# RG-LRU block 2's second half by seven products, and a third head without a block: a change to a hybrid trunk kernel

## The chip, the cores and the metric

The kernel runs on one core of a Trainium2 chip. The metric is the device time of one execution in microseconds (us). The median of three runs of the kernel before is 1455.85 us (1454.58 to 1456.62).

## What is computed

One step of a decoder layer on 2048 prompt tokens and 8 sample tokens of width 1024. In short:

```python
hn = rmsnorm(x, g_norm) * (1 + scale) + shift       # scale, shift, gate from silu(c) @ w_ada + b_ada
xa, za, q, k, v, glr, zg = split(hn @ w_in)
# RG-LRU group, 8 blocks of 128 channels
xc = conv4(xa); gx, ga = sigmoid(blockdiag(xc))      # gates, one 128x128 matrix a block
a = exp(8 * ga * log_sigmoid(lam)); u = sqrt(1 - a*a) * gx * xc
h[t] = a[t] * h[t-1] + u[t]; y_lru = h * silu(za)
# GLA group, 4 heads of 128 keys and 256 values
S[t] = diag(alpha[t]) S[t-1] + k[t]^T v[t]; o[t] = q[t] S[t]
y_gla = rmsnorm_per_head(o) * silu(zg)
x = x + gate * (concat(y_lru, y_gla) @ w_out); y = rmsnorm(x, g_final)
```

All is float32. Results are the outputs of both token groups and the new states (recurrent, convolution, GLA).

## The kernel before

**Precision.** A float32 product is made of three matmuls of split operands: high by high, high by low, low by high. So one projection of 128 columns of w_in on n tokens is 8 x 3 = 24 matmuls of 128 x n (`project`, L661 to L663).

**Two halves.** The 2048 tokens are worked in two halves of 1024. In each half the four GLA heads run in the order HEADS = (3, 0, 1, 2). After a head come the RG-LRU blocks given to it: in the first half all eight (LRU_TILES: block 0, then 1 and 2, then 3 and 4, then 5 to 7), in the second half the first block of each entry of LATE_TILES; blocks 6 and 7 of the second half run with the start of the out-projection. A half is cut into segments of tokens (SEGS): two of 512 in the first half, 384, 384 and 256 with the 8 samples (264) in the second. The samples of a block run with its second half, save for the blocks in EARLY, whose samples run in the first half, in segments of 512, 256 and 264 (SAMPLES; chosen in `xa_load`).

**Seven products.** For the second half's gate columns of three heads (`gates_seven`) and for the blocks in EARLY (`lru_seven`), a pair of 128-column groups on 1024 tokens is not made by `project` but by a seven-product scheme (`seven`): seven products of 12 matmuls of 128x512 each (`product`, L1561) and additions on DVE. The combinations of weights that it needs are made ahead by `pair_weights`, one pair after another, and kept in DRAM (`twd`). This stage stands between the two halves, in the order gates_seven(0), lru_seven(0), gates_seven(1), lru_seven(1), gates_seven(2).

**The order.** The instruction streams of the engines are given by the order in which Python emits them. Each engine executes its stream in order. Work that shall lie beside matmuls is put off: `after(units, fn)` puts a function on a heap, due some units later, and `tick()`, called after every projection or value tile, advances the clock and runs what is due. The GLA's recurrence works so: `chunks` runs one 128-token chunk (`gla_chunk`), and puts off the next by PACE. `new_values` empties the heap of the recurrence's entries before a head's value tiles are written, since the value tiles vh and vl hold one head at a time.

**Background work.** `pair_weights` comes first; after the last pair, `out_weights` makes the combinations for the out-projection in 16 steps (0 to 15): POOL loads r (L829), DVE multiplies and combines (L850), and in some steps b22 and t are split on ACT and DVE into p (L854, L855); POOL stores r, t (L864) and p (L857). Each step puts off the next by 4 units. It pauses at the stage between the halves and goes on after it. The tiles r, t, p and g are in the pool `hp`. After the last head the rest of it is run (`while outw["busy"]`), then the pools `gp` and `hp` are closed, and the out-projection's pools use their places: `load_w` (L1710) loads the first weights by SP, `hi_part` (L1696, ACT) and `lo_part` (L1699, DVE) split them. A tile in a reused place waits for the last readers and writers of what it overlaps.

**A block.** `xa_unit` projects a segment, ACT copies it to xa (L1394), ACT and DVE do the convolution (cv, L1276 and L1278), `split` or the lines after it make xh on ACT and xl on DVE (L1295 and L1296, or L1302 and L1303). Two or three units later `gates` runs six matmuls on xh and xl (L1315 to L1317) with two activations (L1318); after the last segment come ACT's exponentials (L1323 to L1326), DVE's tg, tx (L1331, L1332), the scan over 1024 tokens (L1334) and the sample step. `out` multiplies by silu(za) (L1352) and `spill` stores it (L675, L679). At a head's end `gla_out` transposes the normalized chunks (L1162; L1164 for the samples) and DVE multiplies by the gate (L1167).

The lines of the out-projection's matmuls are L1846. After the change the line numbers rise by 2 to 12.

Of the kernel before, what the change touches and what calls it, by code (L numbers as in the profile page):

```python
# [33 lines left out]
PAD, PAD_XP = 16, 32  # L34
SEGS = (((0, 512), (512, 512)), ((0, 384), (384, 384), (768, 264)))
SAMPLES = ((0, 512), (512, 256), (768, 264))
EARLY = (0, 1)
LATE_TILES = ((2,), (3,), (4,), (5, 6, 7))
HEADS = (3, 0, 1, 2)
LRU_TILES = ((0,), (1, 2), (3, 4), (5, 6, 7))  # L40
PACE = ((1, 1), (1, 0.75, 1.5))
ZB11, ZT1, ZT2, ZB21, ZT3, ZB22, ZT4 = range(7)

CTS = (8, 0)
# [10 lines left out]
def hybrid_kernel(ctx, tc, i, o):  # L55
# [506 lines left out]
    def first_head():  # L562

        h = HEADS[0]
        n = DV + RANK
        v = vh, vl = new_values()

        def evict(tt, ps, low=None):
            hi, lo = vh[tt // 4][:, tt % 4], vl[tt // 4][:, tt % 4]
            S.copy(hi, ps[:, :DV])  # L570
            turn48 = low_rank(ps[:, DV:n], slice(0, P), tt * P, st)

            def lower():
                V.tensor_tensor(lo, ps[:, :DV], hi.bitcast(F32), op=OP.subtract)
            if low is None:
                lower()
            else:
                low.append(lower)
            return turn48

        def second(g, u, low=True):
            x = xt0[4 + 2 * g:6 + 2 * g]
            return apply(turn(x, (2 * u, 2 * u + 1)), 4 + 2 * g, (2 * u, 2 * u + 1), 2, low)

        def pair(a, kts):
            for kt in range(*kts):
                for tt in (a, a + 1):
                    if tt not in begun:
                        begun[tt] = acc()
                    value_mm(begun[tt][:, :n], slice(tt * P, (tt + 1) * P), wv0, n, (kt, kt + 1))  # L590

        with in_order():
            ranks = []
            ss = squares(st, xt0[4:6], P, "junk")
            split_parts(1)
            rs = scales(st, ss, 2)
            split_parts(1)
            times(xt0[4:6], rs)
            low = []
            for tt in range(4):  # L600
                value_mm(begun[tt][:, :n], slice(tt * P, (tt + 1) * P), wv0, n, (6, KT))
                ranks.append(evict(tt, begun[tt], low))
# [24 lines left out]
            second(1, 2)  # L627
            second(1, 3)
            pair(4, (4, KT))
            ranks = [evict(tt, begun[tt]) for tt in (4, 5)]  # L630
            pair(6, (0, KT))
            ranks += [evict(tt, begun[tt]) for tt in (6, 7)]
        store_parts()
        with tc.issue_after(last[V.engine]), tc.issue_after(last[S.engine]):
            normalize(st, [xsr], NS, "junk")

        def rest():
            for f in ranks:
                f()
        return v, prep, rest  # L640
# [57 lines left out]
    pend = []  # L698
    clock = [0, 0]

    def after(units, fn, gla=False, val=False):
        clock[1] += 1
        heapq.heappush(pend, (clock[0] + units, clock[1], fn, gla, val))

    def tick(units=1.0):
        clock[0] += units
# [197 lines left out]
    def sample_values(h, w, n):  # L904

        n4 = n // 4
        vs = gp.tile([P, DV], F32, tag="os", name="vs")
        ps = acc()
        for kt in range(KT):
            raw = w[kt // 4]  # L910
            for g in range(4):
                PE.matmul(ps[32 * g:32 * g + NS, :n4], fs[:, kt], raw[:, kt % 4, g * n4:(g + 1) * n4],
                          start=kt == 0, stop=kt == KT - 1)
        for g in range(4):
            r = slice(32 * g, 32 * g + NS)
            (S.copy if g % 2 else V.tensor_copy)(vs[r, :min(n4, DV - g * n4)], ps[r, :min(n4, DV - g * n4)])
        for g in range(4):
            c = slice(g * n4, min((g + 1) * n4, DV))
            G.dma_start(vsd[h][:, c], vs[32 * g:32 * g + NS, :c.stop - c.start])
        if n > DV:  # L920
            r = slice(96, 96 + NS)
            return low_rank(ps[r, DV - 3 * n4:n4], r, TH)
        return lambda: None

    def new_values():
        while any(e[4] for e in pend):
            e = min(e for e in pend if e[3])
            pend.remove(e)
            heapq.heapify(pend)
            e[2]()  # L930
        return [[gp.tile([P, 4, DV], F32R, tag=tag, name=tag, bufs=2) for _ in range(2)] for tag in ("vh", "vl")]

    def values(half, h, w):
        first = h == HEADS[0]
        n = DV + (RANK if first else 0)
        vh, vl = new_values()
        turns = []
        for tt in range(8):
            if half == 1 and tt == first:
                with held(V) if first else ExitStack():  # L940
                    raw = raw_values(h, n)
            if tt == 4:
                while drips:
                    drip()
            if half == 0 or tt < 6:
                ps = acc()
                value_mm(ps[:, :n], slice(tt * P, (tt + 1) * P), w, n, (0, KT))
            elif tt == 6:
                both = [acc(), acc()]
                for k in (0, 4):  # L950
                    for m in range(2):
                        value_mm(both[m][:, :n], slice((6 + m) * P, (7 + m) * P), w, n, (k, k + 4))
                ps = both[0]
            else:
                ps = both[1]
            hi, lo = vh[tt // 4][:, tt % 4], vl[tt // 4][:, tt % 4]
            S.copy(hi, ps[:, :DV])  # L957
            V.tensor_tensor(lo, ps[:, :DV], hi.bitcast(F32), op=OP.subtract)  # L958
            if len(turns) == 3 or tt == 7 and turns:
                turns.pop(0)()  # L960
            if first:
                turns.append(low_rank(ps[:, DV:n], slice(0, P), tt * P))
            tick(0.5)
        if half == 1:
            turns.append(sample_values(h, raw, n))
        for f in turns:
            after(1, f, True)
        return vh, vl
# [201 lines left out]
    def gla_head(half, h, wv=None, ahead=None):  # L1170
# [15 lines left out]
        def chunks(s, c):  # L1186

            nch = min(SEGS[half][s][1], TH - SEGS[half][s][0]) // P
            if c == 0:
                prep[s, "run"] = gla_start(half, h, s, prep[s])  # L1190
                after(PACE[half][0], lambda: chunks(s, 1), True, True)
                return
            if c == nch and half:
                gate_load(s)
            gla_chunk(half, h, s, c - 1, prep[s], prep[s, "run"], v)
            if c < nch:
                after(PACE[half][1], lambda: chunks(s, c + 1), True, True)
                return
            gla_norm(nch, prep[s, "run"])
            after(PACE[half][2] if half else 1 if s + 1 < ns else 2, lambda: finish(s), True)  # L1200
            if s + 1 < ns:
                after(0, lambda: chunks(s + 1, 0), True, True)
            elif half == 1:
                G.dma_start(o[4][0, 0, h], St[h])

# [22 lines left out]
        for s in range(ns):  # L1228
# [10 lines left out]
            if s + 1 < ns:  # L1239
                dec = gla_decay(half, h, s + 1)  # L1240
            if s == 0:
                after(2 if h == HEADS[0] else 1, lambda: chunks(0, 0), True, True)
            tick()
        if half == 1:
            after(1, lambda: sample(prep[2][3], 0), True)
# [418 lines left out]
            lru_last_a(LRU_TILES[k])  # L1664
    gates_ahead(HEADS[0])
    gates_seven(0)
    for n in range(2):
        lru_seven(n)
        gates_seven(1 + n)
    while drips:  # L1670
        drip()
    close_sp()
    for k, h in enumerate(HEADS):
        wx = []
        gla_head(1, h, ahead=lambda: wx.extend(weights(XA + LATE_TILES[k][0] * P, P)))
        lru(1, LATE_TILES[k][:1], wx)
    flush_gla()
    while outw["busy"]:
        heapq.heappop(pend)[2]()
    gpx.close()  # L1680
    hpx.close()

# [577 lines left out]
```

## Time and profile before

| | us |
|---|---|
| median of 3 runs | 1455.85 |
| profiled execution | 1454.69 |
| its span | 1452.9 |
| PE busy | 1424.1 |
| DVE busy | 1051.5 |
| ACT busy | 689.6 |
| POOL busy | 220.0 |

The span goes from the first to the last instruction that the profiler recorded; 1.8 us of the execution lie around it. PE is TensorE's matmuls, PEld its weight loads, DVE is VectorE, ACT ScalarE, POOL GpSimd, SP SyncE; a q behind an engine's name is its queue, which issues DMAs. A row of a timeline gives start, duration, engine, line, operation, output and inputs, shape, count, and in brackets how long the engine had been idle and what ended it. Matmuls overlap one another: the time that one takes on PE is the distance between starts, not its duration.

The stages by time: first half to about 600 us, the seven products from 603 to 708, the second half to about 1076 (the last head's sample transposes), blocks 6 and 7 to about 1127, then the out-projection to the end.

### The profile page before, as it was taken

The page shows a single profiled execution, that of the slowest core. Times are in us where ns is not written, and L with a number is a line of the kernel's source. Part 1 is how long each engine was busy: PE and PEld are TensorE (multiplying, and loading weights), DVE is VectorE, ACT ScalarE, POOL GpSimd, SP SyncE. Part 2 cuts the span into 40 slices and gives each one's busy share as a digit, 9 for nine tenths or more (in the row PEclk, how much of TensorE's full clock was granted, in tenths as well). Part 3 has the DMA queues.
Part 4 walks back from the last instruction along what each step waited for, and adds up shares of the span by engine and source line. Part 5 has one row for each costly group of instructions (what it writes and reads, how often), then busy time and mean ns, then how long its engine had stood idle before and what let it go on. Part 6 is the DMA issues. An engine that isn't in the chain of part 4 may idle for free. (4 is left out here: it accounts for less than half of the span.)

```text
span 1452.9 us, 23584 instructions
## 1 busy us (share of the span) xinstructions
PE 1424.1 (98%) x8741; PEld 1250.8 (86%) x8741; DVE 1051.5 (72%) x2477; ACT 689.6 (47%) x1251; POOL 220.0 (15%) x364
## 2 busy tenths in 40 slices
PE   7999999999999999999999999999999999999998
PEld 5888989899898988778999999999998887788886
DVE  5757657776676688955468687586788986688886
ACT  4644544662545358524353454535557622144342
POOL 0200111212122113100212322323100000000000
PEclk9999999999999999999999999999999999999999
DMA  9755775764666455667846565656562767694453
GB/s 328 268 185 175 260 262 203 249 236 165 199 209 203 148 179 207 207 221 237 292 158 201 186 217 184 220 186 209 184 226 83 276 221 272 232 362 131 139 171 116
DMA packets 161752, 305.33 MB, mean 210 GB/s; under 512 B 12962, under 2 KB 91458, under 8 KB 159197
## 3 DMA queue, kind: packets, MB, share of 16 engines
q1 hardware_dynamic: 106837, 217.39, 43.6%
q0 software_dynamic: 22752, 70.44, 14.3%
q10 hardware_dynamic: 32048, 16.00, 3.7%
q8 instruction: 69, 1.13, 0.3%
q14 instruction: 46, 0.38, 0.1%
HBM read 188.51 MB, written 115.33 MB: 209 GB/s over the span
## 5 line engine op out<-in xcount | busy, mean ns | idle before, releaser
L661 PE MATMUL acc<-hh,w 128*128 128x512 f32 (+3 forms) x1112 | 386.1, 347 | 0.5 <-DVE xb L999 0.2
L662 PE MATMUL acc<-hl,w 128*128 128x512 f32 (+3 forms) x1112 | 375.6, 338 | 0.2 <-DVE hl L205 0.2
L663 PE MATMUL acc<-hh,w 128*128 128x512 f32 (+3 forms) x1112 | 375.1, 337 | 0.0
L662 PEld LDWEIGHTS acc<-hl,w 128*128 128x128 f32 x1112 | 209.3, 188 | 18.1 <-issue 1.2
L661 PEld LDWEIGHTS acc<-hh,w 128*128 128x128 f32 x1112 | 209.2, 188 | 18.1 <-ACT tx L1318 0.9
L663 PEld LDWEIGHTS acc<-hh,w 128*128 128x128 f32 x1112 | 209.1, 188 | 16.3
L1846 PE MATMUL acc<-w,a 128*128 128x512 f32 (+1 forms) x792 | 184.8, 386 | 0.0
L1846 PEld LDWEIGHTS acc<-w,a 128*128 128x128 f32 x792 | 146.8, 188 | 33.2 <-issue 3.4
L346 PE MATMUL acc<-w,hh 128*128 128x256 f32 (+1 forms) x508 | 144.7, 285 | 0.0
L348 PE MATMUL acc<-w,hl 128*128 128x256 f32 (+1 forms) x508 | 143.5, 282 | 0.2 <-DVE hl L228 0.2
L347 PE MATMUL acc<-w,hh 128*128 128x256 f32 (+1 forms) x508 | 143.4, 282 | 0.0
L1846 PE MATMUL tp<-w,a 128*128 128x512 f32 x564 | 136.0, 391 | 0.0
L1846 PEld LDWEIGHTS tp<-w,a 128*128 128x128 f32 x564 | 105.2, 188 | 26.8 <-issue 5.2
L346 PEld LDWEIGHTS acc<-w,hh 128*128 128x128 f32 x508 | 95.5, 188 | 1.3 <-ACT zs L1128 0.4
L348 PEld LDWEIGHTS acc<-w,hl 128*128 128x128 f32 x508 | 96.2, 189 | 0.4 <-DVE hl L228 0.4
L347 PEld LDWEIGHTS acc<-w,hh 128*128 128x128 f32 x508 | 96.0, 189 | 0.2
L1128 ACT ACTIVATE zs<-acc 128x512 f32<-128x512 f32 (+3 forms) x70 | 34.3, 490 | 107.0 <-PE acc L663 104.0
L1696 ACT CAST a<-s 128x512 fp32r<-128x512 f32 x61 | 36.5, 619 | 96.1 <-issue 36.6
L1278 DVE SCALAR_TENSOR_TENSOR cv<-xa,vecT,cv 128x512 f32<-128x512 f32 (+2 forms) x120 | 76.3, 638 | 7.2 <-ACT cv L1276 6.7
L1129 DVE SCALAR_TENSOR_TENSOR zs<-zs,acc 128x512 f32<-128x512 f32 (+3 forms) x70 | 38.4, 548 | 46.7 <-ACT zs L1128 46.7
L957 ACT CAST vh<-acc 128x256 fp32r<-128x256 f32 x56 | 20.5, 369 | 94.2 <-PE acc L348 81.8
L958 DVE TENSOR_TENSOR vl<-acc,vh 128x256 fp32r<-128x256 f32 x56 | 23.3, 420 | 51.1 <-ACT vh L957 51.1
(403 smaller groups left out, 2746.4 us busy)
## 6 DMA issues: line engine op xcount, KB each, us to landing
parts<-w SPq DMA_DIRECT2D x37, 1024.0 KB
w<-parts SPq DMA_DIRECT2D x28, 1024.0 KB
wr<-in_w_in_dram SPq DMA_DIRECT2D x38, 512.0 KB
a<-mixd SPq DMA_DIRECT2D x63, 256.0 KB
w<-wd SPq DMA_DIRECT2D x12, 1024.0 KB
w<-twd SPq DMA_DIRECT2D x20, 512.0 KB
mixd<-zs ACTq DMA_DIRECT2D x34, 256.0 KB
wada<-in_w_ada_dram SPq DMA_DIRECT2D x16, 512.0 KB
```

The lines of the kernel that those rows point to most:

```text
L346: PE.matmul(ps, hh[:, kt, c], hi[:, kt % 4], start=kt == 0, stop=False)
L347: PE.matmul(ps, hh[:, kt, c], lo[:, kt % 4], start=False, stop=False)
L348: PE.matmul(ps, hl[:, kt, c], hi[:, kt % 4], start=False, stop=kt == KT - 1)
L661: PE.matmul(ps[:, :n], hi[:, kt], a, start=kt == 0, stop=False)
L662: PE.matmul(ps[:, :n], hi[:, kt], b, start=False, stop=False)
L663: PE.matmul(ps[:, :n], lo[:, kt], a, start=False, stop=kt == KT - 1)
L958: V.tensor_tensor(lo, ps[:, :DV], hi.bitcast(F32), op=OP.subtract)
L1128: S.activation(z, ps, AF.Tanh, scale=0.5)
L1129: V.scalar_tensor_tensor(z, z, 1.0, ps, op0=OP.add, op1=OP.mult)
L1278: V.scalar_tensor_tensor(cv[:, cq], xa[:, cq.start + k:cq.stop + k], cw[k], cv[:, cq], op0=OP.mult, op1=OP.add)
L1696: S.copy(t[:, 0, k], (low(t) if src is None else src)[:, k])
L1846: PE.matmul(ps, t[:, u, k], w[:, v, k, c], start=(q < 3 or ps is own) and (k, u, v) == (0, 0, 0), stop=(k, u) == (3, 1), skip_group_check= ...
```

## The change

Four things change together:

- EARLY gets block 2: its second half is made by the seven products, so there are six pairs of weights in place of five, and its samples run in the first half.
- LATE_TILES gives blocks 3, 4, none, and 5 to 7 to the four heads of the second half. The third head (head 1) has no RG-LRU block.
- `new_values` is called for each half of a head's value tiles, and only drains the recurrence as far as that half's place needs: four chunks of the head before for tiles 0 to 3, eight for tiles 4 to 7 (`chunked` counts them). So the last four chunks of a head can stand between the next head's first value tiles. PACE's second half has 0.5 units between chunks in place of 0.75.
- Places: the samples' value tile vs moves from the pool `gp` to `xp`, and a small tile pads `gp` before it is closed.

```diff
-EARLY = (0, 1)
-LATE_TILES = ((2,), (3,), (4,), (5, 6, 7))
+EARLY = (0, 1, 2)
+LATE_TILES = ((3,), (4,), (), (5, 6, 7))
-PACE = ((1, 1), (1, 0.75, 1.5))
+PACE = ((1, 1), (1, 0.5, 1.5))
...
-        vs = gp.tile([P, DV], F32, tag="os", name="vs")
+        vs = xp.tile([P, 512], F32, tag="f512", name="vs")[:, :DV]
...
-    def new_values():
-        while any(e[4] for e in pend):
+    chunked = [8]
+
+    def new_values(v, g):
+
+        while chunked[0] < 4 * g + 4:
             e = min(e for e in pend if e[3])
             pend.remove(e)
             heapq.heapify(pend)
             e[2]()
-        return [[gp.tile([P, 4, DV], F32R, tag=tag, name=tag, bufs=2) for _ in range(2)] for tag in ("vh", "vl")]
+        for x, tag in zip(v, ("vh", "vl")):
+            x.append(gp.tile([P, 4, DV], F32R, tag=tag, name=tag, bufs=2))
...
-        vh, vl = new_values()
+        v = vh, vl = [], []
         turns = []
         for tt in range(8):
+            if tt % 4 == 0:
+                new_values(v, tt // 4)
...
             gla_chunk(half, h, s, c - 1, prep[s], prep[s, "run"], v)
+            chunked[0] += 1
...
             if s == 0:
-                after(2 if h == HEADS[0] else 1, lambda: chunks(0, 0), True, True)
+                chunked[0] = 0
+                after(2 if h == HEADS[0] else 1, lambda: chunks(0, 0), True)
...
-    for n in range(2):
+    for n in EARLY:
         lru_seven(n)
-        gates_seven(1 + n)
+        if n < 2:
+            gates_seven(1 + n)
...
     for k, h in enumerate(HEADS):
-        wx = []
-        gla_head(1, h, ahead=lambda: wx.extend(weights(XA + LATE_TILES[k][0] * P, P)))
-        lru(1, LATE_TILES[k][:1], wx)
+        wx, js = [], LATE_TILES[k][:1]
+        gla_head(1, h, ahead=js and (lambda: wx.extend(weights(XA + js[0] * P, P))))
+        lru(1, js, wx)
     flush_gla()
     while outw["busy"]:
         heapq.heappop(pend)[2]()
+    gp.tile([P, 24], F32, name="pad")
     gpx.close()
     hpx.close()
```

More of the change, by code (lines that the diff above doesn't have):

```diff
@@ L565, in first_head @@
         n = DV + RANK
-        v = vh, vl = new_values()
+        v = vh, vl = [], []
+        for g in range(2):
+            new_values(v, g)
         def evict(tt, ps, low=None):
@@ L699, in hybrid_kernel, with after @@
     clock = [0, 0]
-    def after(units, fn, gla=False, val=False):
+    def after(units, fn, gla=False):
         clock[1] += 1
-        heapq.heappush(pend, (clock[0] + units, clock[1], fn, gla, val))
+        heapq.heappush(pend, (clock[0] + units, clock[1], fn, gla))
     def tick(units=1.0):
@@ L935, in values @@
         n = DV + (RANK if first else 0)
-        vh, vl = new_values()
+        v = vh, vl = [], []
         turns = []
         for tt in range(8):
+            if tt % 4 == 0:
+                new_values(v, tt // 4)
             if half == 1 and tt == first:
@@ L1190, in chunks @@
                 prep[s, "run"] = gla_start(half, h, s, prep[s])
-                after(PACE[half][0], lambda: chunks(s, 1), True, True)
+                after(PACE[half][0], lambda: chunks(s, 1), True)
                 return
@@ L1195, in chunks @@
             gla_chunk(half, h, s, c - 1, prep[s], prep[s, "run"], v)
+            chunked[0] += 1
             if c < nch:
-                after(PACE[half][1], lambda: chunks(s, c + 1), True, True)
+                after(PACE[half][1], lambda: chunks(s, c + 1), True)
                 return
@@ L1201, in chunks @@
             if s + 1 < ns:
-                after(0, lambda: chunks(s + 1, 0), True, True)
+                after(0, lambda: chunks(s + 1, 0), True)
             elif half == 1:
```

## The prediction, made before the run

> **What bounds the kernel now.** I read the page's first two parts, then the table of windows, then the waits of PE, and last the timelines of single engines around the places that the change touches.
>
> ```profile
> span 1452.9 us, 23584 instructions
> ...
> PE 1424.1 (98%) x8741; PEld 1250.8 (86%) x8741; DVE 1051.5 (72%) x2477; ACT 689.6 (47%) x1251; POOL 220.0 (15%) x364
> ...
> PE   7999999999999999999999999999999999999998
> ```
>
> PE is busy for 1424.1 of 1452.9 us, so only 28.8 us of idle PE exist in the whole run. Two things alone can move the time: fewer or shorter matmuls, or more or less of that idle time. The other engines have room on the whole, but not in every stretch:
>
> ```profile
> 0.00:25.00 25.00, 18.39 (x165) 12.80 (x169) 12.50 (x50) 10.37 (x19) 1.32 (x6) 0.93 0.98 322
> ...
> 1075.00:1100.00 25.00, 22.89 (x143) 21.59 (x143) 23.49 (x54) 18.17 (x34) 0.00 (x0) 1.00 0.60 212
> 1100.00:1125.00 25.00, 23.26 (x143) 22.41 (x141) 19.29 (x39) 18.47 (x27) 2.22 (x3) 1.00 0.26 95
> ```
>
> The columns are PE, PEld, DVE, ACT, POOL, then the granted clock. From 1075 to 1125 us, where the last head's samples and RG-LRU blocks 6 and 7 run ahead of the out-projection, PE stands for 2.1 and 1.7 us while DVE is at 23.5 of 25. That stretch has no slack on DVE. The first row serves a rival below.
>
> **The matmuls.** What one costs is the distance between starts, since they are pipelined:
>
> ```profile
> 270.06 0.39 PE L661 MATMUL acc<-hh,w 128*128 128x512 f32 x1
> ...
> 278.22 0.39 PE L1315 MATMUL acc<-xh,wg 128*128 128x512 f32 x1
> ```
>
> ```profile
> 1078.50 0.33 PE L661 MATMUL acc<-hh,w 128*128 128x384 f32 x1
> ...
> 1081.62 0.28 PE L661 MATMUL acc<-hh,w 128*128 128x264 f32 x1
> ...
> 1084.50 0.33 PE L661 MATMUL acc<-hh,w 128*128 128x384 f32 x1
> ```
>
> 36 matmuls of 512 columns start between 270.06 and 278.22: 0.2267 us each. 18 of 384 lie between 1078.50 and 1081.62: 0.1733. 24 of 264 lie between 1081.62 and 1084.50: 0.120, which I take for 256 columns as well.
>
> Block 2's second half now takes two projections (xa and za) of 24 matmuls on each of 384, 384 and 264 columns: 48 x (0.1733 + 0.1733 + 0.120) = 22.40 us. By seven products it is 7 x 12 matmuls of 512 columns: 84 x 0.2267 = 19.04. That is **-3.36**. Its samples move to the first half, where the segments 512, 512 become 512, 256, 264: 48 x (0.2267 + 0.120 + 0.120) - 96 x 0.2267 = 22.40 - 21.76 = **+0.64**. The gates (six matmuls a segment) gain 0.08 in one half and lose it in the other. Matmuls: **-2.7**, which is all that can be gained without touching idle time.
>
> **First half: a new wait at block 2's first gates.** Blocks 1 and 2 follow each other. DVE finishes block 1's chain (tg, tx, scan, outputs) and then the convolution of block 2's first segment; only then can that segment be split into xh and xl, which the gates read.
>
> ```profile
> 267.54 0.59 ACT L1394 COPY xa<-acc 128x512 f32<-128x512 f32 x1 [0.23 <-PE acc L663]
> ...
> 275.77 0.62 ACT L1302 CAST xh<-cv 128x512 fp32r<-128x512 f32 x1 [0.40 <-DVE cv L1278]
> ```
>
> ```profile
> 265.88 1.23 DVE L1331 SCALAR_TENSOR_TENSOR tg<-xl,tg 128x1032 f32<-128x1032 f32 x1 [1.35 <-ACT tg L1326]
> ...
> 269.91 2.28 DVE L1334 TENSOR_TENSOR_SCAN tg<-xl,tx 128x1024 f32<-128x1024 f32 x1
> ...
> 272.17 0.75 DVE L1278 SCALAR_TENSOR_TENSOR cv<-xa,vecT,cv 128x512 f32<-128x512 f32 x1
> ...
> 274.99 0.75 DVE L1278 SCALAR_TENSOR_TENSOR cv<-xa,vecT,cv 128x512 f32<-128x512 f32 x1
> ...
> 276.42 0.69 DVE L1303 TENSOR_TENSOR xl<-cv,xh 128x512 fp32r<-128x512 f32 x1 [0.54 <-ACT xh L1302]
> ```
>
> The first projection of block 2 ends near 267.4 (ACT copies it at 267.54). Two units later come the gates, now at 278.22 (quoted above), 1.1 us after xl is done at 277.11. With the change those two units are the 256 and 264 segments: 48 x 0.120 = 5.8 us instead of 48 x 0.2267 = 10.9, so PE arrives 5.1 us earlier, at 273.1. Nothing ahead of xl in DVE's and ACT's order changes up to there: tg waits for ACT, and the scan, the convolution and the split follow in order. PE can start one matmul (0.23) on xh and then waits for xl: 277.1 - 273.1 - 0.2 = 3.8, less some 0.4 because the 256 segment's work asks less of ACT. I take **+3.4** (2 to 4). The wait is not won back later, since PE is the bound.
>
> **Between the halves and in the second half.** Block 2's seven products enter among gates_seven and lru_seven. The loads use SP as blocks 0 and 1 have them do. One more pair of weights is prepared in the background (POOL loads and stores, ACT and DVE passes); PE doesn't wait for any of it where the page shows PE full. What comes late is the first head's value weights, second part:
>
> ```profile
> 702.61 0.32 SPq L293 DMA_DIRECT2D w<-parts  x1
> ```
>
> ```profile
> 707.85 0.28 PE L346 MATMUL acc<-w,hh 128*128 128x272 f32 x1
> ```
>
> It is issued 5.2 us before the first value matmul and read 1.6 us after that. In the new order one more spill stands ahead of it, and it is issued 1.8 us later against its reader: between 0 and +1.8. Then the second half's heads:
>
> ```profile
> PE tp L1164 <- DVE os L1124: 1.6, 3, 0.5
> PE po L1072 <- DVE on L1081: 1.5, 2, 1.0
> ```
>
> These are PE's largest waits from 709 to 1070 us, 3.1 in all, on the GLA's chunk and sample results. With no RG-LRU block in the third head, its last four chunks run between the next head's value tiles, so DVE gets its chunk work closer together (a loss up to 2 us), and the gates of one block are gone there (a gain up to 1). The shorter pace of 0.5 shifts chunks by a fraction of a unit. For weights and heads together I take **+0.3**, with ends -1 and +3.
>
> **The tail: a new wait ahead of the out-projection.** The combinations of output weights (out_weights) are made in 16 background steps, after the pairs. One more pair pushes them later: with the change the last step, 15, no longer ends in the middle of the last head, but stands in DVE's order behind the last head's sample output. The first out-projection weights (load_w, SP) go to a place that overlaps this step's split tile p; so SP waits until the store of p has landed. ACT's casts of these weights (hi_part) stand **ahead of** block 6's split xh in ACT's order, and PE's gates of block 6 need xh. So: step 15, its store, a 1 MB load, three casts, the split, PE.
>
> ```profile
> 1076.38 0.61 PE L1164 MATMUL tp<-sel,os 128*128 128x8 f32 x4 [1.05 <-DVE os L1124]
> ...
> 1092.82 0.33 PE L1315 MATMUL acc<-xh,wg 128*128 128x384 f32 x1
> ...
> 1094.91 0.44 PE L1315 MATMUL acc<-xh,wg 128*128 128x384 f32 x1 [0.89 <-ACT tx L1318]
> ```
>
> ```profile
> 1076.81 0.89 DVE L1167 SCALAR_TENSOR_TENSOR zs<-tp,gsc,zs 128x264 f32<-128x264 f32 x2 [0.48 <-PE tp L1164]
> 1077.62 0.29 DVE L679 COPY mixs<-zs 128x8 f32<-128x8 f32 x2
> ...
> 1079.08 1.23 DVE L1332 TENSOR_TENSOR tx<-tx,tg 128x1032 f32<-128x1032 f32 x1
> 1080.23 0.61 DVE L1278 SCALAR_TENSOR_TENSOR cv<-xa,vecT,cv 128x384 f32<-128x384 f32 x1
> 1080.76 2.35 DVE L1334 TENSOR_TENSOR_SCAN tg<-xl,hc,tx 128x1024 f32<-128x1024 f32 x1
> ...
> 1083.75 0.55 DVE L1352 SCALAR_TENSOR_TENSOR zs<-tg,zs 128x384 f32<-128x384 f32 x1
> ...
> 1087.37 0.55 DVE L1296 TENSOR_TENSOR xl<-cv,xh 128x384 fp32r<-128x384 f32 x1
> ```
>
> ```profile
> L850 DVE TENSOR_TENSOR r<-r,g x32: 668/684/693, 328.0 to 1014.2; 128x512 f32<-128x512 f32 x32
> ```
>
> ```profile
> L855 DVE TENSOR_TENSOR p<-r,p x8: 415/418/419, 464.2 to 1023.5; 128x256 fp32r<-128x256 f32 x8
> ```
>
> Call T the sample transposes at 1076.38. PE reaches block 6's gates at 1092.82 = T + 16.4. DVE from 1076.81 = T + 0.4: sample output 0.89, copies 0.29, step 15's two products 2 x 0.684, tg and tx 2 x 1.23, scan 2.35, outputs 2 x 0.55, two convolution passes 2 x 0.61, and six passes of 256 columns (four of step 15, two splits of p) 6 x 0.418 = 2.51. Sum 12.2, less 15 overlaps of 0.08 (1079.08 + 1.23 ends 0.08 after the next start): 11.0. So p is split at T + 11.4. Before, p's last store was issued at 1025.9, 45 us ahead of SP's load; now it stands in the chain:
>
> ```profile
> L857 POOL DMA_DIRECT2D wd<-p x32: 540/540/647, 461.2 to 1025.9; - x32
> ...
> DMA to landing us min/median/max: 2.0/3.3/6.7
> ```
>
> ```profile
> 1071.19 0.33 SPq L1710 DMA_DIRECT2D w<-wd  x1
> ```
>
> ```profile
> 1273.05 0.33 SPq L1710 DMA_DIRECT2D w<-wd  x1
> ```
>
> ```profile
> 1279.79 1.14 ACT L1696 CAST w<-w 128x512 fp32r<-128x512 f32 x2 [5.11 <-DMA w<-wd]
> ```
>
> p's stores (L857) take 3.3, between 2.0 and 6.7. SP's load was issued at 1071.19; where ACT is seen waiting for such a load it took 1279.79 - 1273.05 = 6.7. Other transfers share the queues there; in the tail I take 5.8, between 4.8 and 7. It lands at T + 11.4 + 3.3 + 5.8 = T + 20.5. Three casts take 1.6 (1.14 for two), the split and xl (0.55 less the overlap) 0.5 each: block 6's gates go at T + 23.1. PE waits 23.1 - 16.4 = 6.7. The 0.89 that PE waits now at 1094.91 falls inside it, and I count 0.7 of the later waits of this stretch as absorbed while DVE and ACT catch up: **+5.1**. With store and load at their short ends (2.0, 4.8) it is +2.8, at their long ends (6.7, 7) +9.7.
>
> The Trainium skill, "DMA: Bandwidth & Descriptors", section "Anatomy of one DMA — SWDGE (gpsimd) path", fits a transfer to 2.0 us and its bytes by 436 KB per us. An estimate by that page makes the 128 KB store 2.3 us and the 1 MB load 4.4, so the wait would be 2.4 us shorter; the trace's own 3.3 and 6.7 are longer, and the sum goes by them.
>
> **Sum.** -2.7 + 3.4 + 0.3 + 5.1 = **+6.1**. The profiled execution took 1454.69 (its span 1452.9, 1.8 around it): 1460.8. The median of the three runs shown, 1455.85, lies 1.2 higher, which belongs to the range.
>
> **The rivals.**
> *One wait only* (0.15). Either the tail's load is earlier than I think, or block 1's chain is: without the tail +1.0 (1455.7), without the first half's wait +2.7 (1457.4). For it: each hangs on one order of instructions. Against it: both stand in that order, and neither has cover.
> *The products come through* (0.12; the other side). Mechanism: DVE's background passes leave the two chains. In the first half the weight passes between tg and the scan, and in the tail step 15's passes, are what makes xl and p late; if DVE reaches block 1's chain 4 us earlier and p's store lands by T + 7.9, PE waits at neither place: -2.7 + 0.3, or 1452.3. It decides where w's load lands at T + 13.7 instead of T + 20.5. Against it: the row at 265.88 shows DVE idle for 1.35 and waiting for ACT, so its backlog isn't the cause; and step 15 cannot start before T.
> *A long tail* (0.12): store and load at their long ends, or DVE's crowding between value tiles at +2: 1463 to 1468.
> *A colder clock* (0.05). The window from 0 to 25 us was granted 0.93, so a cold start there costs 25 x 0.07 = 1.75 us; every window around 1100 us stands at 1.00 with waits up to 1.7 us. A wait of 6.7 us could cost the same again: 1462.6. The Trainium skill, "TensorE: Matmul & The Clock Gate", section "HAM oscillation — how this bites in real kernels", says that a wait across the activity window throttles the array again. No wait in this trace is long enough to show that.
>
> **How the numbers follow.** The forecast has 0.56, between 1457.6 and 1464. The range is 1453.5 to 1467.5: it leaves out most of the case on the other side and the far end of the long tail, some 0.17. A measurement of this kernel can tell about 0.2% (2.9 us) from no change. Slower by more than that: most of the forecast, the long tail and the clock, 0.68. Within it: the one-wait case and the forecast's lowest part, 0.20. Faster: 0.12.
>
> **What would show it.** PE busy falls by 2 to 3 us while PE idle rises by 7 to 10. Near 273 us PE waits for xl L1313 some 3 to 4 us. In the tail SP's first load_w is issued about 15 us after the sample transposes, ACT waits for it (DMA w<-wd), and block 6's gates start 20 us or more after T. Wrong would be: no wait of PE above 2 us in either place, PE busy not falling, or new waits of the same size in the third head's value tiles.

## The result, and the profile after

The changed kernel takes 1491.58 us (median of 4 runs, 1488.82 to 1495.94) against 1455.59 before (median of 4): a ratio of 1.025, 95% interval 1.0224 to 1.0276. That is 36 us more; 6.1 were forecast. The profiled execution has a span of 1490.2 us against 1452.9: 37.3 us more. The page:

```profile
span 1490.2 us, 23612 instructions
...
PE 1436.1 (96%) x8729; PEld 1256.3 (84%) x8729; DVE 1058.3 (71%) x2488; ACT 692.2 (46%) x1255; POOL 225.3 (15%) x374
...
PE   8999999999999999999999999999978999999998
```

PE's idle time is now 1490.2 - 1436.1 = 54.1 us, against 28.8: **25.3 us more waiting**. And PE's busy time rose by 12.0 us, although its matmuls should need 2.7 us less: **some 14.7 us more for matmuls that were to get shorter**. Where the second part comes from shows in the granted clock. Windows of 10 us of the changed kernel (columns: PE busy, clock, DMA share, GB/s). The one from 1110, where PE waits for most of it, is left out; no other from 130 to 1480 us is below 1.00:

```profile
270.00:280.00 10.00, 6.82 (x38) 0.78 0.88 258
280.00:290.00 10.00, 10.00 (x55) 0.88 0.68 216
920.00:930.00 10.00, 6.92 (x42) 0.71 0.69 238
930.00:940.00 10.00, 10.00 (x84) 0.95 0.16 48
1030.00:1040.00 10.00, 9.73 (x51) 0.83 0.70 252
1090.00:1100.00 10.00, 9.95 (x55) 0.83 0.42 152
...
1120.00:1130.00 10.00, 8.58 (x31) 0.55 0.26 104
1170.00:1180.00 10.00, 6.74 (x24) 0.83 1.03 426
```

Busy time times the missing clock, row by row: 1.5 + 1.2 + 2.0 + 0.5 + 1.7 + 1.7 + 3.9 + 1.1 = 13.6 us. Each of the six places lies at a long wait of PE. The waits of PE from 900 to 1180 us, in the columns of the table of waits (total, times, longest):

```profile
PE acc L1325 <- ACT xh L1305: 8.2, 1, 8.2
PE po L1122 <- DVE xt L1113: 6.0, 2, 3.1
PE acc L1858 <- ACT a L1708: 3.3, 1, 3.3
PE tp L1050 <- DVE xb L1035: 2.7, 1, 2.7
```

With the wait in the first half (3.18, below) these are six waits of 2.7 to 8.2 us, 23.4 together. Before, the largest wait after 130 us was 1.4.

**The first half.** PE and ACT at block 2's first gates:

```profile
273.24 0.28 PE L665 MATMUL acc<-hh,w 128*128 128x264 f32 x1
276.70 0.80 PE L1325 MATMUL acc<-xh,wg 128*128 128x512 f32 x1 [3.18 <-ACT xh L1312]
```

```profile
276.03 0.62 ACT L1312 CAST xh<-cv 128x512 fp32r<-128x512 f32 x1 [0.59 <-DVE cv L1288]
```

PE arrives at 273.5, and block 1's chain on DVE makes it wait, as the prediction had it. What it didn't have is what follows (windows of 1 us):

```profile
274.00:275.00 1.00, 0.00 (x0) 1.00 0.93 197
275.00:276.00 1.00, 0.00 (x0) 0.81 1.00 287
276.00:277.00 1.00, 0.29 (x1) 0.50 1.27 294
277.00:278.00 1.00, 1.00 (x3) 0.50 0.80 263
281.00:282.00 1.00, 1.00 (x4) 0.50 0.07 12
282.00:283.00 1.00, 1.00 (x5) 0.78 0.93 123
283.00:284.00 1.00, 1.00 (x6) 1.00 0.92 270
```

Two us into the wait the clock falls to a half, and it stays there for 6 us after PE has work again.

**The tail.** DVE's last split of p, SP's first load of w, ACT, and PE:

```profile
1108.22 0.43 DVE L857 TENSOR_TENSOR p<-t,p 128x256 fp32r<-128x256 f32 x1 [0.94 <-ACT p L856]
```

```profile
1113.38 0.33 SPq L1722 DMA_DIRECT2D w<-wd  x1
```

```profile
1118.67 1.14 ACT L1708 CAST w<-w 128x512 fp32r<-128x512 f32 x2 [4.38 <-DMA w<-wd]
```

```profile
1112.29 0.34 PE L665 MATMUL acc<-hh,w 128*128 128x384 f32 x1
1120.79 1.01 PE L1325 MATMUL acc<-xh,wg 128*128 128x384 f32 x2 [8.16 <-ACT xh L1305]
```

This is the chain of the prediction, link by link. The sample transposes T stand at 1096.13: p is split at T + 12.5 (forecast 11.4), SP issues at T + 17.3 (14.7), ACT has w at T + 22.5 (20.5), PE goes at T + 24.7 (23.1).

**The samples of the second half's heads.** A wait that no step had, with PE, ACT and POOL near 921 us:

```profile
924.86 1.08 PE L1122 MATMUL po<-xt,qm 128*32 128x256 f32 x8 [3.08 <-DVE xt L1113]
```

```profile
922.53 1.71 ACT L1112 ACTIVATE xt<-xt,smp 128x256 f32<-128x256 f32 x4 [3.54 <-DMA xt<-in_state_gla_dram]
```

```profile
915.54 1.44 POOL L831 DMA_DIRECT2D r<-in_w_out_dram  x2 [2.50 <-DMA wd<-r]
916.97 0.78 POOL L1108 DMA_DIRECT2D xt<-in_state_gla_dram  x1
```

POOL's queue holds a background step's load of r, which waits 2.50 us for the stores of the step before; the load of the samples' state stands behind it.

**The out-projection's start.** The third load of w, and who waits for it:

```profile
1159.48 0.32 SPq L2133 DMA_DIRECT2D a<-mixd  x1
...
1160.85 0.38 SPq L1722 DMA_DIRECT2D w<-wd  x1
```

```profile
1169.17 2.18 ACT L1708 CAST w<-w 128x512 fp32r<-128x512 f32 x4 [9.30 <-DMA w<-wd]
```

Before, this load was issued 10 us ahead of the first product, at 1118.34; now it is issued 1.6 us after the first product (1159.3), because a load of a ahead of it in SP's order waits for PE's last projection.

### The profile page after: what moved, and what is told of

Same layout as the page of the kernel before. It is cut to its first block, busy times and chain, and to the rows that moved or that the text cites. A ratio compares the mean times of both kernels' runs of the same rounds, so it can differ in the third digit from the quotient of the medians.

```text
span 1490.2 us, 23612 instructions
## 1 busy us (share of the span) xinstructions
PE 1436.1 (96%) x8729; PEld 1256.3 (84%) x8729; DVE 1058.3 (71%) x2488; ACT 692.2 (46%) x1255; POOL 225.3 (15%) x374
## 4 chain that ended last, share of the span: by engine, by line
PE 58%; DVE 15%; issue 11%; DMA 7%; ACT 7%; POOL 2%; POOLq 0%; SPq 0%; DVEq 0%; ACTq 0%
PE acc L1858 10%; PE tp L1858 7%; PE acc L663 7%; PE acc L665 7%; PE acc L664 7%; PE acc L1571 7%; PE acc L346 2%; PE acc L347 2%; PE acc L348 2%; DMA w<-wd 1%; DMA xt<-in_state_gla_dram 1%; PE po L1084 1%; DVE cv L1288 1%; DVE tg L1344 1%; ACT L989 1%
## 5 line engine op out<-in xcount | busy, mean ns | idle before, releaser
L663 PE MATMUL acc<-hh,w 128*128 128x512 f32 (+3 forms) x1080 | 375.9, 348 | 1.3 <-DVE mid L1015 1.1
L664 PE MATMUL acc<-hl,w 128*128 128x512 f32 (+3 forms) x1080 | 365.0, 338 | 0.2 <-DVE hl L205 0.2
L665 PE MATMUL acc<-hh,w 128*128 128x512 f32 (+3 forms) x1080 | 364.5, 337 | 0.0
L663 PEld LDWEIGHTS acc<-hh,w 128*128 128x128 f32 x1080 | 204.8, 190 | 19.2 <-DVE mid L1015 1.4
L664 PEld LDWEIGHTS acc<-hl,w 128*128 128x128 f32 x1080 | 205.2, 190 | 16.8 <-DVE hl L205 0.5
L665 PEld LDWEIGHTS acc<-hh,w 128*128 128x128 f32 x1080 | 204.7, 190 | 16.4 <-issue 0.4
L966 DVE TENSOR_TENSOR vl<-acc,vh 128x256 fp32r<-128x256 f32 x56 | 23.4, 421 | 53.7 <-ACT vh L965 53.6
```

The lines of the kernel that those rows point to most:

```text
L663: PE.matmul(ps[:, :n], hi[:, kt], a, start=kt == 0, stop=False)
L664: PE.matmul(ps[:, :n], hi[:, kt], b, start=False, stop=False)
L665: PE.matmul(ps[:, :n], lo[:, kt], a, start=False, stop=kt == KT - 1)
```

## The experiments

All ratios are against the kernel before, run on the same chip. Edits are to the changed kernel where nothing else is said. The changed kernel's own runs lie 7 us apart, so a difference of 5 us says little by itself; which waits go and which stay in the trace says more.

**fill_waits.** Idle matmuls in four of the waits; the results are not used.

```diff
+    FILL = {(0, 2): 12, (1, 6): 40, 0: 20, 2: 20}
+    def fill(ps, count, n):
+        for _ in range(count):
+            PE.matmul(ps, hh[:, 1, :P], hh[:, 0, :n], start=True, stop=True)
...
+                    if s == 0 and g == 0 and (half, j) in FILL:
+                        fill(ps, FILL[half, j], sn)
...
+        if b0 and h in FILL:
+            fill(po, FILL[h], DV)
```

> The changed kernel with idle matmuls put into four of PE's long waits, whose results nothing reads (they go to the PSUM tile that the next real matmul starts afresh): 12 of 512 columns ahead of block 2's first gates in the first half (the 3.18 us wait at 273), 20 of 256 ahead of the sample output of heads 0 and 2 (3.08 us at 921, 2.91 us at 1087), 40 of 384 ahead of block 6's first gates (8.16 us at 1112). The waits at 1026 (2.69 us) and 1170 (3.26 us) are left as they are, to compare. No wait of DVE, ACT or DMA is taken away, and the four waits go on ending at the same moment. Theory (the long waits cost twice: the wait itself, and half a clock after it, which comes because PE stood idle for some 2.5 us or more): the four half-clock stretches go, which cost 2.8, 3.2, 1.9 and 4.1 us of PE's time, the two others stay: about 1491.6 - 12 = 1480, granted clock up from 0.985 to about 0.993. Rival (the lower clock has another cause, such as the load on the chip, and only stands near the waits): the time stays at 1490 to 1493 and the clock at 0.985.

Measured: 1487.36 us, clock 0.993. The windows at the first two filled waits:

```profile
270.00:280.00 10.00, 9.13 (x55) 7.61 (x54) 10.00 (x25) 4.84 (x8) 0.91 (x1) 1.00 0.89 262
280.00:290.00 10.00, 10.00 (x67) 9.18 (x66) 6.12 (x13) 5.35 (x13) 2.03 (x3) 1.00 0.79 252
920.00:930.00 10.00, 9.02 (x79) 8.20 (x78) 7.45 (x26) 8.29 (x14) 0.76 (x1) 1.00 0.61 199
930.00:940.00 10.00, 10.00 (x91) 10.00 (x90) 9.97 (x22) 3.17 (x6) 3.27 (x7) 1.00 0.36 113
```

The clock stays at 1.00 at both, with nothing else changed. The fourth head's first value matmul starts at 978.41 in this kernel and at 984.24 in the changed one: 5.8 us won, where 2.8 + 3.2 = 6.0 were expected. So half the loss at these waits is the clock, and it comes from PE's idleness. Behind that point the run missed: 4 us in all, not 12. The added matmuls changed the order in which DVE's instructions were laid down near 1093, where the sample transposes now wait 3.7 us for block 5's scan step (stT). So the tail's share is not shown by this run.

**gates_later.** Block 2's first gates a unit later.

```diff
-                after(3 if j == LRU_TILES[3][-1] or half == 1 and j != LRU_TILES[3][0] else 2, lambda: gates(t, [s]))
+                after(3 if j == LRU_TILES[3][-1] or half == 1 and j != LRU_TILES[3][0] or half == 0 and j == 2 and s == 0 else 2, lambda: gates(t, [s]))
```

> The changed kernel with block 2's first gates of the first half put off by three units in place of two, so that its first za segment (24 matmuls of 512 columns, 5.4 us) stands ahead of them. Theory (the wait at 273 us comes from the two short segments that bring PE 5.1 us earlier to these gates): the 3.18 us wait and the half clock behind it (2.8 us) go, and the time falls by about 6, to 1485.5; the waits after it (1.3 at 327, 1.0 at 335) may go as well, another 2. Rival (DVE is behind for good in this stretch, and the wait only moves to the next reader): the time falls by less than 2.

Measured: 1486.76 us. The wait and its clock are gone (a 1.2 us wait at the next segment's gates is new); 4.8 us instead of 6. The two waits at 324 and 333 stayed.

**steps_three_units.** Background steps faster.

```diff
-            after(4, lambda: step(s, r, g))
+            after(3, lambda: step(s, r, g))
```

> The changed kernel with out_weights' steps following each other after 3 units in place of 4, so that step 15 ends about 60 us ahead of the last head's sample output. Theory (the tail's 8.16 us wait ahead of block 6's gates is the chain step 15, store of p, load of w): this wait and the half clock behind it (4.1 us) go, 12 us, and with them perhaps the 3.26 us wait at 1170; the steps meet the recurrence at other places, so the waits at 921 to 1087 change by up to 6 us either way: 1474 to 1482. Rival (block 6's gates wait for DVE's own chain of block 5 and the samples, and the weights' load is only the last of several late things): the wait falls by less than 4 us and the time stays above 1485.

Measured: 1477.12 us, 14.5 less. PE's waits from 1080 to 1160 in this kernel:

```profile
PE acc L1858 <- ACT a L1708: 3.0, 1, 3.0
PE po L1122 <- DVE xt L1113: 2.3, 1, 2.3
PE acc L1325 <- DVE zs L1137: 1.4, 1, 1.4
```

The 8.2 us wait is gone: the tail's chain is as forecast. With its clock it cost some 12 us by the changed kernel's rows (8.2 of wait, 3.9 of clock), more than twice its forecast. The rest of the 14.5 us lies elsewhere: the wait for xb near 1026 is 1.6 us here, with no lower clock behind it. The wait at the out-projection's start stays, so it has another cause.

**drain_all.** The old order of the recurrence.

```diff
-        while chunked[0] < 4 * g + 4:
+        while chunked[0] < 8:
```

> The changed kernel, but with all eight chunks of the head before done ahead of a head's value tiles, as before the change (the empty third head, block 2 by seven products and the pace of 0.5 stay). Theory (the long waits come from the positions of the background steps and of the segments, not from where the last chunks stand): the waits at 273, 1112 and 1170 stay; those at 921, 1026 and 1087 change by a few us; the time lies within 5 us of 1491.6. Rival (the late chunks crowd DVE between the value tiles, and the samples' chain waits behind them): the waits at 921 to 1087 go, and the time falls by 8 to 14.

Measured: 1486.03 us, between the two. The waits at 273, 921, 1107 and 1164 stay (3.2, 3.3, 8.5, 3.2); the wait of 2.7 for xb at 1026 goes, and the one of 2.9 for the samples' state at 1087 falls to 1.1.

**recurrence_only.** The kernel before with the recurrence's part alone: EARLY, LATE_TILES and the loop of lru_seven put back in the changed kernel.

> The kernel before with the recurrence's part of the change alone: value tiles drained by halves, pace 0.5, vs in the other pool and the pad; EARLY and LATE_TILES as before, so no new pair of weights, no moved samples and an RG-LRU block in each head. Theory (the change's cost comes from block 2's move, through the positions of segments and background steps; late chunks alone cost little): 1454 to 1460. Rival (late chunks between the value tiles crowd DVE and cost some 5 us wherever they stand): 1460 to 1466.

Measured: 1455.86 us, ratio 0.9993 (0.9984 to 1.0003). This part costs nothing by itself.

**block_only.** drain_all and the pace of 0.75.

> The changed kernel without the recurrence's part: all eight chunks drained ahead of the value tiles and a pace of 0.75, so that block 2 by seven products, its samples in the first half and the empty third head are left. Theory (the waits at 273, 1112 and 1170 and their clock come from block 2's move alone): 1483 to 1488, the three waits within 0.5 us of 3.2, 8.3 and 3.3. Rival (the pace of 0.5 brings them about): below 1475.

Measured: 1485.12 us, ratio 1.0196 (1.0172 to 1.022). Block 2's move with the empty third head makes four fifths of the loss. The three waits are 3.2, 7.9 and 3.1, and one of 2.7 for the samples' state stands near 921.

**samples_moved.** The kernel before, with one line:

```diff
-            t.samples = (j in EARLY) == (half == 0)
+            t.samples = (j in (0, 1, 2)) == (half == 0)
```

> The kernel before with one thing of the change: block 2's samples run in the first half, in segments of 512, 256 and 264, and its second half is made by projections on 512 and 512 columns, without samples. No seven products for it, no sixth pair of weights, the old LATE_TILES. PE's matmuls stay equal to 0.1 us (+0.64 in the first half, -0.64 in the second). Theory (the first half's loss of 8.3 us in the changed kernel, that is a 3.2 us wait at 273, the half clock after it and small waits behind, comes from these segments alone): 1455.9 + 6 to 9 = 1462 to 1465, the wait at 273 between 3.0 and 3.4 us. Rival (it comes from the sixth pair's passes on DVE): within 2 us of the kernel before.

Measured: 1463.5 us, ratio 1.0061 (1.004 to 1.0083): with no matmul added or taken away, the smaller segments alone cost 8.5 us, with a wait of 3.2 us at block 2's first gates. The kernel also waits up to 2.3 us for samples in later heads, so not all of it lies in the first half.

**swapped_places.** The first a tiles of the out-projection in other places.

```diff
-    free[:] = range(4, 12)
+    free[:] = [6, 7, 4, 5, 8, 9, 10, 11]
```

> The changed kernel with the a tiles of the out-projection's start handed out in another order (6, 7, 4, 5 in place of 4, 5, 6, 7), so that the first loads of a go to a place whose last reader is block 7's xa weights and not, as since the change, the weights of its very last za projection. (The move of block 2 takes weights tiles out of the second half, so the ring of three weights buffers stands elsewhere at its end.) Theory (SP waits with these loads for PE's last projection, and the load of w that stands behind them comes 20 us later than before, so that ACT's casts and PE's products wait for it): the 3.26 us wait at 1170 and its half clock (1.5) go, and the time falls by 4 to 7, to 1485 to 1488. Rival (w's load is late because the whole tail is): less than 2 us.

Measured: 1482.78 us, 8.8 less, somewhat over the 4 to 7 expected, with runs that lie 9 us apart (and 4.7 where it is added to three repairs, below; there the ratios are 1.0119 and 1.0107, with intervals that overlap). SP's third load of w in this kernel:

```profile
1145.70 0.32 SPq L1722 DMA_DIRECT2D w<-wd  x1
```

It is 15 us earlier than in the changed kernel, and PE's wait at the out-projection's start is gone. So this cause is the places. By the order of the kernel's calls, block 2's move takes two weights tiles out of the second half, the ring of three weights buffers ends one buffer on, and the places that were laid out for the old end now wait for the last projection.

**three_repairs, repairs_later_load, four_repairs, five_repairs.** gates_later, steps_three_units and drain_all together; then, beside them, the load of r a unit later; then the three with the swapped places; then these with the second sample load on ACT's queue:

```diff
-        G.dma_start(s0, i["state_gla"][0, b0:b0 + 4, h].rearrange("b k v -> k b v"))
+        (S if b0 else G).dma_start(s0, i["state_gla"][0, b0:b0 + 4, h].rearrange("b k v -> k b v"))
```

> The changed kernel with three repairs together: block 2's first gates a unit later, background steps after 3 units, all chunks drained. Theory (three separate causes, 5.0, 14.5 and 5.5 us by the single runs): 1491.6 - 25 = 1466.6, 1464 to 1469, no PE wait above 3.5 us. Rival (the causes overlap, since a wait taken away in one place comes back in the next): above 1472.

> The same three repairs, but each background step's load of r is put off by one unit, and the step comes two units after the load, so that POOL doesn't stand waiting for the stores of the step before (2.5 us at 913) with the samples' state load queued behind it. Theory (the 3 us waits for the sample output come from POOL's order): the waits of PE for xt fall below 1.5 us, and the time is 2 to 6 below the three repairs' own run. Rival (the state's transfer itself is long, and POOL's wait is hidden): within 2 us of that run.

> The three repairs (block 2's first gates a unit later, steps after 3 units, all chunks drained) and the swapped places. Theory: 1474.6 - 6 = 1468.6, between 1466 and 1471. Rival (the out-projection's start then waits for something else): 1473 to 1476.

> The four repairs, and the second load of a head's sample state issued by ACT's queue in place of POOL's, so that it can't stand behind a background step's load of r. Theory (POOL's order is what makes PE wait 3.3 us for the sample output at 917): that wait falls below 1.5 us and the half clock behind it goes, 2 to 4 us below the four repairs' run. Rival (the transfer itself is slow, or the wait is for PE's own sample output ahead of it): within 1.5 us of that run.

Measured: 1474.57, 1473.92, 1469.88 and 1460.96 us. The three repairs gave 17 of the 24.8 us that they gave singly, so they overlap, and the expectation missed. The later load did nothing: r's load still stood ahead of the state's and waited 2.47 us. ACT's queue settled it: 8.9 us where 2 to 4 were expected, at the wait near 917 and at its like in the last head. What stands ahead of the load is not always a background step: near 917 it is one, but in the four repairs' last head the steps are done, and the load stands in POOL's queue behind a load of zs that waited 16.1 us for a store. And some 1.7 of the 8.9 us is a lower clock at 1032 in the four repairs, behind a wait of 1.5 us that the five repairs have as well. Five repairs have a ratio of 1.0043 (1.0027 to 1.0058). PE, and its clock in 40 slices:

```profile
span 1457.2 us, 23617 instructions
...
PE 1423.3 (98%) x8729; PEld 1246.0 (86%) x8729; DVE 1057.7 (73%) x2488; ACT 692.4 (48%) x1255; POOL 222.2 (15%) x370
...
PEclk9999999999999999999999999999999999999999
```

With the long waits the clock losses are gone too: PE is busy for 1423.3 us, 0.8 less than before the change. That leaves 33.9 us idle (1457.2 - 1423.3), 5.1 more than before: near 280, 322 and 331 in the first half, 1.2 to 1.4 us each, and 1.8 for the value weights,

```profile
PE acc L346 <- DMA w<-parts: 1.8, 2, 1.5
```

the one late load that the prediction had, at its upper end.

**five_late_chunks, half_units, half_units_late.** The five repairs with the change's own recurrence order; the five repairs with block 2's short segments counted as half units in place of the later gates; both.

```diff
-                tick()
+                tick(0.5 if half == 0 and j == 2 and s else 1)
...
-            tick()
+            tick(0.5 if half == 0 and t.j == 2 and s else 1)
```

> The five repairs with the change's own recurrence order (value tiles drained by halves) in place of all chunks drained. Theory (the late chunks cost only through the background steps and loads that they met, so with those repaired they neither cost nor gain): within 2 us of the five repairs, 1459 to 1463. Rival (late chunks crowd DVE by themselves): 1464 to 1468.

> The five repairs, but block 2's 256 and 264 segments of the first half count as half a unit each, in place of the gates put off by a unit: the block then takes four units as before the change, so its gates come after the first za segment and the background passes of pair_weights meet the heads where they did before. Theory (what is left of the first half's loss, two waits of 1.5 us near 322 and 331 and one of 1.4 at 280, comes from background passes that moved two units against the matmuls): these waits fall below 0.8 us and the time is 2 to 4 us below the five repairs, 1457 to 1459, and within 0.3% of the kernel before. Rival (DVE is late by block 2's samples and third segment themselves): within 1 us of the five repairs.

> The same with the change's own recurrence order. Theory: the sum of the two effects, 1456 to 1461; it would be the change with all five causes undone and nothing of it left out, and as PE's matmuls are 2.7 us shorter than before, it may reach the kernel before. Rival: above 1463.

Measured: 1464.69, 1465.07 and 1463.46 us, ratios 1.0055, 1.0059 and 1.0049, with intervals that overlap one another's and the five repairs' own. Late chunks can't be told from drained ones here. The half units missed: the waits at 280 and 331 went, but one of 5.1 us (PE tp from DVE xb, at 322) came in their place. All these waits end on DVE, so it seems that DVE is behind in this stretch and that other units only choose which reader meets it; no run shows this by itself. What would repair these last 5 us stays open; no version here beats the kernel before.

## Why the prediction was right in sign and wrong in size

- **Matmuls, -2.7.** PE's busy time in the five repairs, where no clock is lost, is 0.8 below the kernel before. Busy time counts modelled ends, so this bears out a small gain and doesn't measure it.
- **First half, +3.4.** Right in its mechanism: the wait is 3.18, and samples_moved shows that the segments alone make it. (All of it stands at xh; one matmul on xh and then a wait for xl was forecast.) The statement that it "is not won back" was too mild: the half clock behind it took another 2.7, and 1.3 and 1.0 came at 327 and 335.
- **The tail, +5.1.** Right link by link; the wait is 8.16 where 6.7 stood, since DVE and the store were 2.6 us later together and the load and ACT's part 1 us shorter. (The load took 5.3 us from SP's issue to ACT's cast, where 5.8 stood. The estimate of 4.4 beside it was worked out with a fit for POOL's path, and SP issues this load.) The step that failed is the deduction behind it: I counted 1.6 us of later waits as absorbed. Of these the 0.89 went, but 0.5 for xl came and the 1.4 for zs stayed (1.49). And the clock fell to a half (3.9 us); steps_three_units, which takes the chain away, gave 14.5 us, some 12 of them here.
- **Heads, +0.3.** This step failed as a whole. It put the new pair's background work at nothing since PE "doesn't wait for any of it where the page shows PE full", and followed the later steps of out_weights only into the tail. A full PE shows that nothing was late before, not that another order of a queue is harmless. In POOL's queue the loads of the samples' state, which PE waits for, came to stand behind other work: near 917 behind a step's load of r. The two waits took 3.1 and 2.9 us, and 2.5 and 1.7 us in clock behind them; five_repairs shows the cause with 8.9 us. The late chunks, for which a loss of up to 2 us was allowed, took 2.7 us at 1026 and 1.7 in clock. drain_all took that away; without block 2's move, in recurrence_only, no such wait stands (its longest for xb is 1.0).
- **Left out: places.** I followed the one place that the tail's first load waits for, and not the ring of weights buffers, which turns with every tile that is taken out. swapped_places: 8.8 us; by the changed kernel's rows the wait took 3.3 and its clock 1.1, and the rest is no more than the spread of the runs.
- **The rivals.** "One wait only" and "the products come through" fell: both waits came, each by the order that the prediction named. The long tail's 1463 to 1468 was passed by far.
- **The colder clock** was a rival with a chance of 0.05 and a price of 1.75, for one place. It was the second largest term of the result, after the waits themselves: six places, 13.6 us by the windows. I put a low chance on it because no wait in the trace before seemed long enough to show it. But the forecast itself held waits of 3.4 and 6.7 us, more than twice and more than four times as long as the longest that the trace had shown to be harmless (1.4 us; the 1.7 of the prediction is the sum of PE's waits in the window from 1100). And the trace before does show it: the 0.93 of its first 25 us, read as a cold start, is a clock that fell to a half behind two short waits, of 0.46 and 1.31 us:

```profile
10.00 1.07 PE L493 MATMUL pa<-wada,sc 128*32 128x128 f32 x30 [1.31 <-DMA wada<-in_w_ada_dram]
```

```profile
11.00:12.00 1.00, 0.92 (x12) 1.00 1.11 362
12.00:13.00 1.00, 0.86 (x4) 0.63 1.07 399
13.00:14.00 1.00, 1.00 (x16) 0.50 1.05 428
```

On the clock, the Trainium skill, "TensorE: Matmul & The Clock Gate", section "What's actually happening", says that the array returns to half its clock after an idle window of some 3.4 us, and that the window runs freely. This case agrees with the free window and the size, and shows that shorter waits are enough: 2.69 us at 1026 was, while 2.49 us in gates_later and 3.34 us in drain_all, both near 920, left the clock at 1.00. drain_all's windows there:

```profile
920.00:930.00 10.00, 6.66 (x61) 1.00 0.77 255
930.00:940.00 10.00, 9.49 (x81) 1.00 0.16 48
```

When a wait is enough, the traces say too. In each of the 17 traces of this case, the times at which the granted clock changes lie whole steps of 3.413 us apart: in the changed kernel it falls at 275.62, 924.15, 1029.97, 1091.41, 1115.30 and 1173.33, which is 190, 31, 18, 7 and 17 steps from one to the next. Cut from 130 to 1440 us, the 17 traces have 6452 such steps at a clock of 1.00. In 37 of them PE stood idle for 1.76 us or more, and after each of these the next step ran at 0.50. Of the other 6415 only four were followed so, each with 1.5 us of idle time ahead of the sample transposes. So what decides is not the length of a wait but how much of it falls into one step: about half a step is enough. drain_all's 3.34 us lay across the border of two steps, and PE was idle for 1.7 us in each:

```profile
920.33:923.74 3.41, 1.75 (x15) 1.00 0.59 198
923.74:927.15 3.41, 1.73 (x17) 1.00 0.82 298
```

Where the steps lie against the work differs from one execution to the next. So for a wait between some 1.8 and 3.4 us the half clock is chance, which fits the four runs of the changed kernel lying 7 us apart, and the four of the kernel before 2.

## What to carry to other kernels

Where an edit shifts units of work, list for each queue what now stands ahead of what, for each ring of buffers where it ends, and for each place who read it last; an edit that takes tiles out moves all of them, even far from itself. On a PE-bound kernel, price a new wait of more than some 1.8 us with the half clock that can follow it (1.1 to 3.9 us here); shorter ones were rarely followed by it. A background task is free only as long as nothing urgent shares its queue.

## What the runs showed of the hardware that I had not expected

The granted clock fell to 0.50 between 2.1 and 4.3 us after the start of a wait of PE, at 1026 and 1087 only when PE had work again, and came back after 3 to 8 us of work. It did so at all six waits of 2.7 us and more of the changed kernel, but not at every such wait of the others: its changes lie on the fixed steps of 3.413 us, and a step counts by PE's idle time in it. Idle matmuls into a PSUM tile that the next matmul starts afresh kept it at 1.00 at the two waits where fill_waits could show it, and as they ended 0.4 us before the wait did, they made PE no later there. A wait of only 1.5 us can be followed by a lower clock as well: in half_units the 10 us from 1025 had 0.86 with the same wait (tp from os) that left the five repairs at 1.00, where it lay across the border of two steps.
